# Next layer's modulation columns in the first feed-forward: another start, another order, one buffer

## The chip, the cores and the metric

The kernel runs on one core of a Trainium2 chip. The core has several engines with a queue of instructions each, worked off in order: TensorE (matrix products; PE in the profile, PEld for its weight loads), VectorE (DVE), ScalarE (ACT), GpSimd (POOL) and SyncE (SP, which here only issues transfers). Transfers between the large memory (HBM) and the on-chip memory run on 16 DMA engines, and are issued from the queues of SP and POOL. The metric is the time of one execution in microseconds (us), the median of several runs; smaller is better.

## The reference

Two layers of a diffusion backbone are computed for 512 latent tokens (x) and 256 context tokens (ctx), width 1024, in float32. Layer 0 mixes tokens by windowed attention, layer 1 by retention. Each layer ends with a gated feed-forward (SwiGLU, inner width 2816). Each layer is modulated: a condition vector is multiplied by a 1024 x 6144 matrix, and the six parts of the product shift, scale and gate the streams.

```python
for i in range(DEPTH):
    need_ctx_out = i < DEPTH - 1
    mx = jnp.split(c_act @ ada_w[i] + ada_b[i], 6, axis=-1)     # latent stream
    mc = jnp.split(cc_act @ ada_w[i] + ada_b[i], 6, axis=-1)    # context stream
    h_x = modulate(rms_norm(x, norm1_g[i]), mx[0], mx[1])
    h_c = modulate(rms_norm(y_ctx, norm1_g[i]), mc[0], mc[1])
    ...
    x = x + mx[2] * out_x
    x = x + mx[5] * swiglu(modulate(rms_norm(x, norm2_g[i]), mx[3], mx[4]), ffn_w_in[i], ffn_w_out[i])
```

In the last layer the context is not written any more. So layer 1 needs parts 0 and 1 (shift and scale ahead of the mixer) for both streams, and parts 2 to 5 for the latent stream alone. With 128 columns on the 128 partitions, a part is 8 columns of 128 values. That makes 16 columns for two streams and 32 for one.

## The kernel before

Activations lie with the width on the partitions. Each matrix product is done in three float32 products of split operands: a weight tile (128 x 1024 values, `wraw`) is rounded into a high part by a copy on ScalarE (`whi`, L165) and the rest is a subtraction on VectorE (`wlo`, L166, and L141 in `next_w`).

**The first feed-forward** (layer 0, L846 to L1085) works on both streams together, 768 tokens, as two halves of 384. Its inner width is cut into 22 tiles, f = 0 to 21, in groups of 2, 4, 4, 4, 4 and 4. The first two tiles are plain products. From f = 2 on `seven` computes a tile by seven products of half-size blocks instead of eight (L835, twelve matmuls of 384 columns each, into the banks X, Y and Z). Ahead of the products it prepares three pairs of split weights and one smaller pair (`bhi`, `blo`), with four additions on the raw weights (L960 to L966). Behind the products stand additions of the blocks (L977, L985, L987), the gate (L107, L908) and the split of the result (`act`, L165, L166).

After the first tile of a group, `output` multiplies the group before by the second weight matrix (L148 to L150): for each of the 8 blocks of 128 columns the latent stream into a bank `pj` and the context into a bank Z. VectorE adds the gated result to the stream (L253). The last group's `output` comes at the very end with `final` set, and also squares the streams for the next norm (L207 to L210).

**The modulation columns of layer 1** are computed on the side, by VectorE. `ada_tile` (L263) takes one column: POOL's queue issues the transfer of the column's weights (128 x 1024 values, 512 KB, L268). For each stream that needs it, one instruction on VectorE multiplies them by the activated condition row (`crow`: the first 1024 values for the latent stream, the second 1024 for the context) and sums along the row (L271, output `y`, a short readout of the sum behind it). A two-stream column has one transfer and two such reductions, a one-stream column one of each.

The columns wait in the list `ada_q`; `ada_next` (L946) takes one when called. It is called

- in `seven`, behind the split of its weights (from f = 3 on, when the condition rows are there),
- after `seven`, behind the split of its result, except in the first tile of a group,
- in an `output` that isn't final, after each second block of the latent stream, so four times.

That gives 4 calls in the output at f = 2, two each in f = 3, 4 and 5, and then in each group of four one in the first tile, four in its output and six in the three other tiles: 54 calls in all, for 48 columns.

**What sets the order.** The program is written for a framework that tracks which instruction needs which tile of memory, sets the waits, gives out buffers, and fixes the order of each engine's instructions when the program is built, by the order in which they are written and by a model of their times. `after` adds an edge that keeps an instruction behind another one on the same engine; each reduction has one, to the instruction named above. On the chip each engine then takes its instructions in that fixed order: if one waits, all behind it on that engine wait.

Memory is given out by name: `adaw` has one buffer in the pool of the feed-forward, so the next transfer into it can be issued only when the last reduction that reads the old weights is done. When fewer than 32 columns are left, and their number is odd, the weights go into the second half of `crow` instead, which is not read any more then. The same `adaw` buffer holds a weight part before (f = 1) and after (third weight tile of the final output, `spare_w`, L1001).

After the first feed-forward `fold_gain` (L114) joins parts of the modulation with the norms' gains for layer 1.

Of the kernel before, what the change touches and what calls it, by code (L numbers as in the profile page):

```python
# [16 lines left out]
KT = D // P  # L17
# [32 lines left out]
def dit_kernel(ctx, tc, xT, cT, crow, small, consts, masks, tabs0, tabs1, jtab, adaQ, adaN, adaT, wst, out):  # L50
# [11 lines left out]
    def T(pool, cols, tag, bufs, dt=F32):  # L62
        return pool.tile([P, cols], dt, tag=tag, bufs=bufs, name=tag)
# [27 lines left out]
    def after(ins, others):  # L91
        for o in others:
            tc.add_manual_dep(ins.ins, o.ins.name, order, reason="table set turn")
# [42 lines left out]
    def next_w(pool, own=2, raw=None):  # L136

        raw = raw or w_raw()
        hi, lo = w_parts(pool, own)
        nc.scalar.copy(hi, raw)  # L140
        nc.vector.tensor_tensor(lo, raw, hi, op=sub)  # L141
        return hi, lo
# [112 lines left out]
    def cond_rows(pool):  # L255

        cr = T(pool, 2048, "crow", 1)
        nc.sync.dma_start(cr, crow.broadcast_to([P, 2048]))
        for i in range(2):
            silu(cr[:, i * 1024:(i + 1) * 1024], cr[:, i * 1024:(i + 1) * 1024])  # L260
        return cr

    def ada_tile(l, part, d, streams, cr, behind, room, w=None):  # L263

        j = part * 8 + d
        if w is None:
            w = T(room, 1024, "adaw", 1 if l else 3)
        (nc.gpsimd if l else nc.sync).dma_start(w, adaT[l, j])  # L268
        for s in streams:
            junk = T(rp, 1024, "y0", 1, BF16) if l else T(room, 1024, "junk", 1, BF16)  # L270
            after(nc.vector.tensor_tensor_reduce(junk, w, cr[:, s * 1024:(s + 1) * 1024], 1.0,  # L271
                                                 sm_t[:, C_ADAB + l * 48 + j:C_ADAB + l * 48 + j + 1], mult, add,
                                                 mods[l, s][:, part, d:d + 1]), behind)
# [525 lines left out]
    cres = load_stream(1)  # L799
    At.close()  # L800
    AK.close()
    PLAIN = 2
    WIDE = SX + SC
    THIRDS = (slice(0, 384), slice(384, WIDE))
    E = ExitStack()
# [4 lines left out]
    for d4 in range(0, KT, 4):  # L810
        w = [next_w(wo_p) for _ in range(4)]
        if d4 == 0:
            cr = cond_rows(wo_p)
# [38 lines left out]
    fp = F.enter_context(tc.tile_pool(name="fp", bufs=1, reuse_waits="tile"))  # L852
# [42 lines left out]
    def last_sum():  # L895
        for k in range(4):
            S[4, k] = parts(quarter())
            split(park[:, k * 384:(k + 1) * 384], *S[4, k])
# [47 lines left out]

    def ada_next(behind):

        if ada_q:

            w = cr[:, 1024:2048] if len(ada_q) < 32 and len(ada_q) % 2 else None
            ada_tile(*ada_q.pop(0), cr, [behind], fp, w)

    def seven():
        g, u = raw_turn(), raw_turn()
# [13 lines left out]
        if cr:  # L969
            ada_next(half)  # L970
# [36 lines left out]
    def output(acts, final):  # L1007
        gsz = len(acts)
        nd = 1024 // (gsz * P)
        w = []  # L1010

        def one(s, res, c, d):
            while len(w) * nd <= d:
                w.append(spare_w() if final and len(w) == 2 else next_w(fp, 1, raw_turn()))
            wd = w[d // nd]
            o = bank("Z")[:, 0:SC] if s else pj()
            for k in range(gsz):
                c0 = k * nd * P + (d % nd) * P
                mm3(o, (wd[0][:, c0:c0 + P], wd[1][:, c0:c0 + P]),
                    (acts[k][:, c], acts[k][:, c.start + WIDE:c.stop + WIDE]), k == 0, k == gsz - 1)  # L1020
            ins = gated_add(s, 0, 5, d, o, res)
            if cr and not final and s == 0 and d % 2:
                ada_next(ins)
            if final:
                square_and_stats(s, d, res[d])

        if final:
            for st in streams:
                for d in range(KT):
                    one(*st, d)  # L1030
        else:
            for d in range(KT):
                for st in streams:
                    one(*st, d)
# [7 lines left out]
            nc.sync.dma_start(w[k], adaN[u, k // 2][:, k % 2 * 512:k % 2 * 512 + 512])  # L1042
        return ada_unit(u, w, pj, columns)

    ada_q = [(1, part, d, (0, 1)) for part in (0, 1) for d in range(KT)]
    ada_q += [(1, part, d, (0,)) for part in (2, 3, 4, 5) for d in range(KT)]
    wsel[0] = 0
    raws = [0]
    cr = None
# [5 lines left out]
    f, prev = 0, None  # L1055
    for gsz in FFN_GROUPS:
        acts = []
        for i in range(gsz):
            if f < PLAIN:
                acts.append(first[f])  # L1060
                if f == 1:
                    ends.pop(0)()
            else:
                if f == PLAIN:
                    last_sum()
                a, end = seven()
                acts.append(a)
                if f == PLAIN:
                    ends.pop(0)()
                    cr = cond_rows(fp)  # L1070
                if i or f == PLAIN + 2:
                    ada_next(end)
            if i == 0 and prev is not None:
                output(prev, False)
            f += 1
        prev = acts
# [181 lines left out]
    for hd in range(RH):  # L1258
# [211 lines left out]
        w = []  # L1470
# [70 lines left out]
    fp = F.enter_context(tc.tile_pool(name="fp", bufs=1, reuse_waits="tile"))  # L1541
# [88 lines left out]
    f, prev = 0, None  # L1630
    for gsz in FFN_GROUPS:
        acts = []
        for i in range(gsz):
            if f < 2:
                acts.append(first[f])
            elif f == 2:
                w = [next_w(fp), next_w(fp)]
# [153 lines left out]
```

## Time and profile before

| What | us |
|---|---|
| Time, median of 3 runs | 1789.98 |
| lowest and highest run | 1786.59 and 1791.28 |
| Span of the profiled execution | 1794.1 |
| busy in it: PE, VectorE, ScalarE, POOL | 1728.8, 1357.8, 841.7, 134.9 |
| one reduction of a modulation column, mean | 1.279 |

The page gives no time of the profiled execution beside its span; the span lies 4.1 us above the median of the three runs. The profile has several views. The page names the busy time of each engine. The windows view gives busy time by stretch of the span, with the granted clock of TensorE (PEclk, 1.00 is full). The groups of instructions give the line, the engine, what is written from what, how many; busy time and mean; and then the engine's idle time just before them with the instruction that ended it (`<-`). The timeline has single instructions: start, duration, engine, line, and in brackets the idle time before and what ended it. The chain of waits follows the work that ended last back from step to step, with the start and length of each. Times are us from the start of the span unless marked as ns.

### The profile page before, as it was taken

What the parts mean: (1) busy time and instruction counts of PE and PEld (TensorE: products, weight loads), DVE (VectorE), ACT (ScalarE), POOL (GpSimd) and SP (SyncE); (2) the same over time, 40 slices, a digit from 0 to 9 for tenths busy, and PEclk for the clock granted to TensorE, in tenths of its full rate; (3) what the DMA queues carried; (4) which work ended last, traced back from release to release, by engine and by line L of the source; (5) the groups of instructions that cost most, each with busy time, mean ns of one, the idle gap of its engine ahead of it and who ended that gap; (6) DMA issues with size and microseconds to landing.
All of it is one profiled execution on the core that took longest, in us unless ns stands there. A gap on an engine that the chain in (4) does not pass through costs nothing.

```text
span 1794.1 us, 27599 instructions
## 1 busy us (share of the span) xinstructions
PE 1728.8 (96%) x10852; PEld 1535.8 (86%) x10852; DVE 1357.8 (76%) x2365; ACT 841.7 (47%) x1477; POOL 134.9 (8%) x275
## 2 busy tenths in 40 slices
PE   6899999999989999999999999999999999999999
PEld 4777776789889999999988788888897899999998
DVE  6697777688878868686689867758758798777774
ACT  5476666456232425252455534534524465445432
POOL 0035334000000000000010000000000000000000
PEclk9999999999999999999999999999999999999999
DMA  9510002434444534342233533434433323333322
GB/s 339 228 36 25 24 1 83 150 108 154 124 125 130 162 107 153 118 153 83 83 107 106 166 105 110 162 95 134 152 115 117 96 71 106 95 112 112 89 89 83
DMA packets 59890, 206.68 MB, mean 115 GB/s; under 512 B 6640, under 2 KB 7024, under 8 KB 59504
## 3 DMA queue, kind: packets, MB, share of 16 engines
q1 hardware_dynamic: 52848, 179.75, 31.3%
q0 software_dynamic: 6912, 25.17, 4.6%
q8 instruction: 85, 1.39, 0.3%
q14 instruction: 45, 0.37, 0.1%
HBM read 202.80 MB, written 2.10 MB: 114 GB/s over the span
## 4 chain that ended last, share of the span: by engine, by line
PE 73%; DVE 12%; DMA 6%; ACT 4%; issue 2%; POOL 2%; SPq 0%; ACTq 0%; DVEq 0%; POOLq 0%
PE Y L835 13%; PE Z L835 6%; PE pj L148 6%; PE pj L150 6%; PE pj L149 6%; PE Y L1180 4%; PE Z L1193 4%; PE X L835 3%; DMA wraw<-in_wst_dram 2%; DVE wlo L166 2%; PE pj L1193 2%; PE pT L707 2%; DMA adaw<-in_adaT_dram 2%; PE pO L719 2%; PE S L684 2%
## 5 line engine op out<-in xcount | busy, mean ns | idle before, releaser
L165 ACT CAST whi<-wraw 128x1024 fp32r<-128x1024 f32 x177 | 185.1, 1050 | 286.0 <-PE Z L150 70.3
L166 DVE TENSOR_TENSOR wlo<-wraw,whi 128x1024 fp32r<-128x1024 f32 x177 | 215.9, 1222 | 43.4 <-ACT whi L165 43.4
L835 PE MATMUL Y<-aq,whi 128*128 128x384 f32 x640 | 175.6, 338 | 6.1 <-ACT whi L165 4.1
L253 DVE SCALAR_TENSOR_TENSOR res<-pj,mod,res 128x512 f32<-128x512 f32 (+1 forms) x112 | 81.5, 729 | 69.5 <-PE pj L150 68.6
L141 DVE TENSOR_TENSOR wlo<-wraw,whi 128x1024 fp32r<-128x1024 f32 x80 | 98.1, 1227 | 38.0 <-ACT whi L140 37.3
L835 PEld LDWEIGHTS Y<-aq,whi 128*128 128x128 f32 x640 | 117.6, 189 | 8.2 <-ACT whi L165 5.1
L140 ACT CAST whi<-wraw 128x1024 fp32r<-128x1024 f32 x80 | 84.0, 1050 | 81.6 <-DMA wraw<-in_wst_dram 26.8
L835 PE MATMUL Y<-aq,wlo 128*128 128x384 f32 x320 | 108.0, 338 | 1.1 <-DVE wlo L166 1.1
L101 ACT ACTIVATE pr<-pr,stat,qs 128x513 f32<-128x513 f32 (+2 forms) x96 | 74.2, 775 | 31.7 <-DVE stat L691 30.9
L1193 PE MATMUL Z<-whi,sA 128*128 128x512 f32 x256 | 81.0, 392 | 0.6 <-ACT whi L165 0.6
L698 POOL TENSOR_SCALAR pr<-pr,stat 128x512 f32<-128x512 f32 (+2 forms) x96 | 67.2, 714 | 88.8 <-DVE stat L695 66.5
L271 DVE CUSTOM_DVE_ANT_0 y<-adaw,crow,small_sb 128x1024 bf16<-128x1024 f32 x48 | 61.4, 1279 | 12.0 <-DMA adaw<-in_adaT_dram 12.0
L148 PE MATMUL pj<-ax,whi 128*128 128x512 f32 x176 | 68.7, 390 | 0.2 <-DVE res L253 0.2
L150 PE MATMUL pj<-ax,whi 128*128 128x512 f32 x176 | 68.7, 390 | 0.0
L149 PE MATMUL pj<-ax,wlo 128*128 128x512 f32 x176 | 68.5, 389 | 0.0
L707 PE MATMUL pT<-const_sb,pr 128*128 128x128 f32 x352 | 58.8, 287 | 9.9 <-POOL pr L698 7.6
L148 PE MATMUL pj<-act,whi 128*128 128x512 f32 x168 | 66.5, 396 | 0.5 <-DVE res L253 0.5
L149 PE MATMUL pj<-act,wlo 128*128 128x512 f32 x168 | 65.9, 392 | 0.0
L150 PE MATMUL pj<-act,whi 128*128 128x512 f32 x168 | 65.5, 390 | 0.0
L707 PEld LDWEIGHTS pT<-const_sb,pr 128*128 128x128 f32 x352 | 39.6, 142 | 30.2 <-POOL pr L698 18.5
L685 DVE CUSTOM_DVE_ANT_0 pr<-S,mask,qs 128x256 f32<-128x256 f32 (+1 forms) x96 | 53.1, 567 | 15.3 <-PE S L684 8.9
L835 PEld LDWEIGHTS Y<-aq,wlo 128*128 128x128 f32 x320 | 60.6, 189 | 1.8 <-DVE wlo L166 1.8
(520 smaller groups left out, 5277.3 us busy)
## 6 DMA issues: line engine op xcount, KB each, us to landing
wraw<-in_wst_dram SPq DMA_DIRECT2D x238, 512.0 KB, 3.6
adaw<-in_adaT_dram POOLq DMA_DIRECT2D x32, 512.0 KB, 4.3
wx<-in_wst_dram SPq DMA_DIRECT2D x24, 512.0 KB, 4.6
adan<-in_adaQ_dram SPq DMA_DIRECT2D x16, 512.0 KB, 7.5
adan<-in_adaN_dram SPq DMA_DIRECT2D x16, 512.0 KB, 8.8
crow<-in_adaT_dram POOLq DMA_DIRECT2D x16, 512.0 KB, 4.4
res<-in_xT_dram SPq DMA_DIRECT2D x16, 256.0 KB, 5.6
adaw<-in_adaT_dram SPq DMA_DIRECT2D x8, 512.0 KB, 4.1
```

The costliest lines, as they stand in the source:

```text
L101: ins = nc.scalar.activation(*args, **kw)
L140: nc.scalar.copy(hi, raw)
L141: nc.vector.tensor_tensor(lo, raw, hi, op=sub)
L148: nc.tensor.matmul(o, whi, xhi, start=first, stop=False)
L149: nc.tensor.matmul(o, wlo, xhi, start=False, stop=False)
L150: return nc.tensor.matmul(o, whi, xlo, start=False, stop=last)
L165: nc.scalar.copy(hi, t)
L166: return nc.vector.tensor_tensor(lo, t, hi, op=sub)
L253: return nc.vector.scalar_tensor_tensor(res[d], o, mods[l, s][:, part, d:d + 1], res[d], mult, add)
L707: nc.tensor.transpose(tp[:, a * P:(a + 1) * P], self.pr[(0, 2, 1, 3)[a]][:, ki * P:(ki + 1) * P], ident)
L835: nc.tensor.matmul(o, p, r, start=first and k + i == 0, stop=k == 3 and i == 2, skip_group_check=not first)
L1193: ins = nc.tensor.matmul(o, p, r, start=first and k + i == 0, stop=k == 3 and i == 2, skip_group_check=not first)
```

## The change

Three things change in the first feed-forward; the columns computed stay the same 48.

1. `ada_next` does nothing while f < 4. Of the 54 calls, the four in the output at f = 2 and the two in f = 3 fall away; 48 are left, and the last column is taken behind f = 21, just ahead of the final output.
2. The list is filled in another order: not 16 two-stream columns and then 32 one-stream ones, but sixteen times two one-stream columns (parts 2 to 5) and one two-stream column (parts 0 and 1). The last column of the list is a two-stream one.
3. All columns use the buffer `adaw`; none goes to the second half of `crow`, which the context reductions now read until the end.

```diff
-    PLAIN = 2
+    PLAIN, ADA_FROM = 2, 4
...
     def ada_next(behind):
 
-        if ada_q:
-
-            w = cr[:, 1024:2048] if len(ada_q) < 32 and len(ada_q) % 2 else None
-            ada_tile(*ada_q.pop(0), cr, [behind], fp, w)
+        if ada_q and f >= ADA_FROM:
+            ada_tile(*ada_q.pop(0), cr, [behind], fp)
...
-    ada_q = [(1, part, d, (0, 1)) for part in (0, 1) for d in range(KT)]
-    ada_q += [(1, part, d, (0,)) for part in (2, 3, 4, 5) for d in range(KT)]
+    ada_q = []
+    for i in range(2 * KT):
+        ada_q += [(1, 2 + (2 * i + e) // KT, (2 * i + e) % KT, (0,)) for e in range(2)]
+        ada_q.append((1, i // KT, i % KT, (0, 1)))
```

## The prediction

> **What bounds the kernel now.** I read the page first: its busy shares name TensorE, so the question is where TensorE is not busy.
>
> ```profile
> span 1794.1 us, 27599 instructions
> PE 1728.8 (96%) x10852; PEld 1535.8 (86%) x10852; DVE 1357.8 (76%) x2365; ACT 841.7 (47%) x1477; POOL 134.9 (8%) x275
> ```
>
> A share over the whole span hides stages, so next I cut the first feed-forward into stretches: 440 to 531 us holds the first output and the tiles f = 3 to 6, 531 to 841 the rest of the modulation work, 841 to 889 the last tiles, in which no modulation column is left.
>
> ```profile
> core 0: us, PE busy (x) PEld busy (x) DVE busy (x) ACT busy (x) POOL busy (x), PEclk, DMA share, GB/s
> 440.00:531.00 91.00, 81.98 (x440) 75.76 (x439) 75.43 (x120) 32.78 (x53) 5.29 (x10) 0.96 0.37 114
> 531.00:577.00 46.00, 46.00 (x266) 42.13 (x265) 39.55 (x62) 11.73 (x16) 3.17 (x6) 1.00 0.37 120
> 577.00:841.00 264.00, 264.00 (x1520) 252.17 (x1520) 200.07 (x300) 96.44 (x149) 16.41 (x31) 1.00 0.44 134
> 841.00:889.00 48.00, 48.00 (x274) 47.09 (x273) 31.39 (x45) 24.18 (x38) 0.00 (x0) 1.00 0.27 77
> ```
>
> From 531 us on PE is busy in every microsecond: nothing can be gained there, only lost. In the first stretch it is idle for 91.00 - 81.98 = 9.0 us, and there the clock is below 1. Who ends those gaps, by groups of PE instructions in that stretch:
>
> ```profile
> L835 PE MATMUL Y<-aq,whi 128*128 128x384 f32 x128 | 37.0, 350 | 6.1 <-ACT whi L165 4.1 <-ACT hn L975 1.5 <-ACT sq L984 0.4
> L835 PE MATMUL Y<-aq,wlo 128*128 128x384 f32 x64 | 22.5, 351 | 1.1 <-DVE wlo L166 1.1
> L835 PE MATMUL Z<-aq,whi 128*128 128x384 f32 x35 | 10.0, 344 | 1.3 <-ACT sq L982 1.3
> L148 PE MATMUL pj<-act,whi 128*128 128x512 f32 x18 | 7.7, 426 | 0.5 <-DVE res L253 0.5
> L271 DVE CUSTOM_DVE_ANT_0 y<-adaw,crow,small_sb 128x1024 bf16<-128x1024 f32 x20 | 25.6, 1280 | 7.0 <-DMA adaw<-in_adaT_dram 7.0
> ```
>
> 6.1 + 1.1 + 1.3 + 0.5 is all of the 9.0. The names are ScalarE and VectorE, but ScalarE is 36% busy in the stretch (32.78 of 91.00), so it is late because its own inputs are. The last row is VectorE's: 20 modulation reductions, 25.6 us of work, and 7.0 us in which VectorE stood still for the modulation weights. The chain of waits, in order of time, shows one link of it:
>
> ```profile
> 504.81 1.20 DVE y L271
> 506.31 6.68 DMA adaw<-in_adaT_dram
> 513.01 1.28 DVE y L271
> 514.30 0.47 DVE sq L985
> 514.77 1.20 DVE y L271
> 516.27 3.94 DMA adaw<-in_adaT_dram
> 520.23 1.28 DVE y L271
> 521.53 1.15 DVE wlo L166
> 522.72 0.69 PE Y L835
> ```
>
> Two reductions end, only then is the one buffer refilled, VectorE runs into the next reduction and waits in order, and the weight split (wlo) that TensorE needs stands behind it. What the wait costs on PE:
>
> ```profile
> 519.85 0.44 PE L835 MATMUL Y<-aq,whi 128*128 128x384 f32 x1 [2.65 <-ACT whi L165]
> 521.58 0.69 PE L835 MATMUL Z<-aq,whi 128*128 128x384 f32 x1 [1.30 <-ACT sq L982]
> 520.50:527.20 6.70, 5.17 (x15) 4.67 (x16) 5.64 (x7) 2.46 (x5) 0.53 (x1) 0.51 0.40 111
> ```
>
> After gaps of 2.65 and 1.30 us the granted clock is 0.51 for 6.7 us. PE was busy for 5.17 us of that; at full clock the same work takes 5.17 x 0.51 = 2.6, so 2.5 us more are lost.
>
> **The change part by part.** *The late start.* No column is taken before f = 4. That removes from the first output (f = 2) four columns and from f = 3 two, all for two streams: 12 reductions at 1280 ns, 15.4 us of VectorE, and six transfers on POOL's queue, which all come later instead. The other four columns of the stretch (f = 4 and f = 5, eight reductions) become one-stream columns in three cases. Without any reduction VectorE's work in the stretch is 75.43 - 25.6 = 49.8 us; f = 4 and f = 5 put back 1 + 1 + 2 + 1 = 5 reductions, 6.4 us (f = 6 one more). That is 56 us of work beside 80 us of TensorE work, so the cover is there. Of the 9.0 idle us I count 8.6 as going: the 0.4 behind sq L984 stays, since it comes from the activation of the condition rows, ahead of it on ScalarE and waiting for its own transfer. With the gaps the drop of the clock goes, 2.5. Gain 11.1.
>
> ```profile
> 439.69 2.01 ACT L107 ACTIVATE crow<-crow 128x1024 f32<-128x1024 f32 x2 [2.33 <-DMA crow<-in_crow_dram]
> ```
>
> What is late next there? The weight transfers: in the same stretch VectorE also waited once for a raw weight.
>
> ```profile
> DVE wraw L960 <- DMA wraw<-in_wst_dram: 1.8, 1, 1.8
> ```
>
> It may show again; between nothing and half of the 9.0 (4.5) of the idle may stay, and I take 1.0, nearer the lower end, since a single 1.8 us wait on VectorE is all that the rows show beside the modulation.
>
> *The mixed order, and 48 calls up to the end.* Total reductions stay 64, transfers 48. They now go at 4/3 reductions a call instead of one (before: two, then one), and six columns fall on f = 19 to 21, where none was (eight reductions, 10.2 us). In a tile of two calls (f = 4, 5, and the three after each output) there are two or three reductions. Before, with two:
>
> ```profile
> 581.15:595.71 14.56, 14.56 (x86) 14.56 (x85) 12.90 (x20) 7.33 (x12) 1.06 (x2) 1.00 0.51 147
> 581.15:595.71 14.56, 2.58 (x4) 1.00 0.51 147
> 624.87:658.29 33.42, 33.42 (x193) 29.49 (x192) 22.93 (x35) 5.62 (x7) 1.59 (x3) 1.00 0.37 110
> ```
>
> The first row is one seven-product tile, 14.56 us of unbroken PE with VectorE at 12.90; the second is the reductions alone, 2.58 for two. A third brings VectorE to 14.2, still under 14.56. Three such tiles after an output hold eight reductions at most: 3 x 12.90 + 2 x 1.29 = 41.3 of 43.7. The third row is an output: four calls and 22.93 of 33.42, where 1.3 reductions more do nothing. How far may VectorE be late inside a tile? The tight place is the weight split after the last product:
>
> ```profile
> 593.63 4.16 PE Y L835 x24
> 599.87 2.08 PE Y L835 x12
> 597.27 1.23 DVE L166 TENSOR_TENSOR wlo<-wraw,whi 128x1024 fp32r<-128x1024 f32 x1 [0.34 <-ACT whi L165]
> 598.88 1.28 DVE L271 CUSTOM_DVE_ANT_0 y<-adaw,crow,small_sb 128x1024 bf16<-128x1024 f32 x1
> ```
>
> That split ends at 598.5 and PE uses it at 599.87: 1.4 us to spare, with the reduction behind it. So I take the arithmetic of the mixing as hidden: 0, bounds 0 and 3 us (0.25 for each of the twelve tight tiles).
>
> *One buffer.* The second place (the unused half of the condition rows) goes. POOL's queue then waits at every column for the reduction before it, and the only other work of that queue comes in the final output. VectorE waits only if it comes to a reduction before its transfer has landed.
>
> ```profile
> adaw<-in_adaT_dram POOLq DMA_DIRECT2D x16, 512.0 KB, 3.9
> DMA to landing us min/median/max: 3.7/4.4/7.4
> ```
>
> The first row is for 445 to 577 us, the second for 577 to 832. From the end of a reduction to the issue it takes 0.3 us (506.00 to 506.31 above), so a turn is 4.7 us at the median. Two calls in a tile: 2 x 4.7 + 2.67 x 1.29 + 0.2 for the instruction within a pair = 13.0 us of 14.56. With two-stream columns alone, as before: 2 x 4.2 + 4 x 1.28 + 2 x 0.47 = 14.5, even with the shorter landing: that is why the early stretch was bound by this chain, and the mixed order isn't. Cost 0 at the median; it is the first rival's price above it.
>
> *The end.* A pair of reductions now lies between the last tile and the final output.
>
> ```profile
> 888.07 0.55 DVE L166 TENSOR_TENSOR act<-sq,act 128x384 fp32r<-128x384 f32 x1
> 889.28 0.75 DVE L253 SCALAR_TENSOR_TENSOR res<-pj,mod,res 128x512 f32<-128x512 f32 x1 [0.66 <-PE pj L150]
> 889.95 1.22 DVE L166 TENSOR_TENSOR adaw<-wraw 128x1024 fp32r<-128x1024 f32 x1
> 891.12 0.75 DVE L253 SCALAR_TENSOR_TENSOR res<-pj,mod,res 128x512 f32<-128x512 f32 x1
> 578.96 0.24 DVE L114 SCALAR_TENSOR_TENSOR acol<-mod,gm 128x8 f32<-128x8 f32 x2
> ```
>
> The pair (2.6 us) can begin when the split at 888.07 is through, and end at 891.2. If it goes ahead of the gated add at 889.28, that is late by 1.9 us, and its bank was wanted for the third column block about 891: up to 1.5 us of PE. If it goes behind, nothing. I take 0.8, the middle. The last row is the next layer's folded gains, done at 579 us before; they now wait for this last pair: two instructions, 0.24 us, during the final output, after which they are first used.
>
> **Sum.** 8.6 + 2.5 - 1.0 - 0 - 0 - 0.8 = 9.3 us less: 1794.1 becomes 1784.8 in the profiled execution. That execution lies 4.1 us above the median of the runs shown (1789.98), so I carry the difference: 1780.7.
>
> On the clock, the Trainium skill ("TensorE: Matmul & The Clock Gate", Part 1) says that TensorE falls to half clock after about one idle window of 3.4 us and needs a busy one to come back. The trace agrees in kind: 3.95 us of gaps with one matmul between, then 0.51. By the page one window at half clock costs an estimated 1.7 us instead of 2.5, and the sum would be 8.5.
>
> **The rivals.** *The single buffer becomes the bound (slower).* Place: the 14 tiles with two calls. For it: the 6.68 us transfer above, a turn of 7.0 with its issue, and the 7.0 us of waits with this same buffer. Against it: both medians, and that the two-stream columns from 531 to 577 us, on one buffer, cost PE nothing (46.00 of 46.00). With a turn x the cycle is 2x + 3.6; it passes 14.56 at x = 5.5. My gain is used up near 5.8, slower by over 0.3% needs 6.0. At 6.3 it is 16.2, so 1.64 x 14 = 23 us: 1804.
>
> The Trainium skill ("Trainium Kernel Development and Optimization", Best Practices) advises double-buffering to overlap transfers with computing. It speaks against this part; the trace bears it out for two-stream columns in tiles of seven products (7.0 us), not between outputs.
>
> *The gap moves instead of closing.* f = 4 to 6 still use the single buffer, with three reductions in f = 5, and weights for f = 4 come no sooner. If half the idle stays (4.5), no matmul gap reaches the length that dropped the clock, sevens lose 1.5 and the end 1.0: 11.1 - 7.0 = 4.1 less, 1785.9, within what can be told from no change. For it: DMA already served f = 4 late once (1.8 us). Against it: VectorE has 24 us of room.
>
> *The early gap isn't due to the modulation at all,* only labelled so because those reductions happen to stand in order there: then nothing is gained, and the end and the sevens cost 0.8 to 3: 1791 to 1793. Against it stands the chain, in which a landing releases every second link.
>
> **How the numbers follow.** 0.3%, some 5.4 us, is about what a measurement of this kernel can tell from no change. Likeliest case 0.71 (1777 to 1784.5 by its own bounds: 11.1 gained and a run spread of 2, against 4.5 - 1.0 more left over); gap moved 0.12; not due 0.04; single buffer 0.13, mostly over 1795. So faster 0.71, same 0.16, slower 0.13. The range reaches from 1776 to 1789: it takes in the moved gap and leaves out the slow rival and the third.
>
> **What would show it.** Right: PE without gaps over 0.5 us from 443 us to the end of the first feed-forward, clock 1.00 there, VectorE 55 to 60 us busy in the 80 us after 440, the final output beginning about 10 us earlier. The first part is wrong if PE gaps between the first output and tile 7 still sum to over 4 us; the mixing and the one buffer are wrong if VectorE's idle time before the reductions exceeds some 10 us in total and PE has gaps after 531 us; the end, if PE has a gap over 1.5 us in the final output.

## The result and the profile after

| | before | changed |
|---|---|---|
| median of 4 runs each | 1790.63 us | 1778.32 us |
| lowest and highest | 1786.59 and 1793.67 | 1777.24 and 1782.69 |
| ratio, with its 95% interval | | 0.9935 (0.9915 to 0.9956) |
| profiled execution: time, span | span 1794.1 | 1777.24, 1775.5 |

The change makes the kernel 12.3 us faster by the medians; 9.3 were forecast. The page of the changed kernel begins:

```profile
span 1775.5 us, 27602 instructions
PE 1717.1 (97%) x10852; PEld 1527.1 (86%) x10852; DVE 1356.0 (76%) x2365; ACT 841.2 (47%) x1477; POOL 134.4 (8%) x275
```

VectorE does the same work (1356.0 against 1357.8), PE has the same 10852 matmuls. By stretches, the same three as before and the 80 us for which the prediction named a load:

```profile
core 0: us, PE busy (x) PEld busy (x) DVE busy (x) ACT busy (x) POOL busy (x), PEclk, DMA share, GB/s
440.00:531.00 91.00, 90.99 (x522) 87.08 (x522) 70.80 (x107) 34.61 (x56) 3.17 (x6) 1.00 0.35 109
531.00:577.00 46.00, 46.00 (x270) 44.00 (x269) 37.27 (x56) 15.51 (x24) 3.17 (x6) 1.00 0.34 106
577.00:841.00 264.00, 263.15 (x1514) 250.65 (x1513) 207.53 (x314) 94.33 (x147) 16.36 (x31) 1.00 0.43 132
440.00:520.00 80.00, 79.99 (x462) 77.51 (x462) 64.09 (x97) 33.56 (x55) 2.65 (x5) 1.00 0.34 104
```

In the first row the 9.0 us of idle PE and the low clock are gone, and the number in brackets says more than the busy time: 522 matmuls start in these 91 us, where 440 did before. In the third row PE now has 0.85 us of gaps, where it had none. The groups of VectorE's instructions from 430 to 880 us show what the single buffer does:

```profile
L271 DVE CUSTOM_DVE_ANT_0 y<-adaw,crow,small_sb 128x1024 bf16<-128x1024 f32 x64 | 81.9, 1279 | 33.7 <-DMA adaw<-in_adaT_dram 33.5
```

VectorE stands still for modulation weights for 33.5 us, against 12.0 on the page before. The waits are up to 5.6 us long; here are two, one early and one late, from the timeline (start, duration, and in brackets the idle time):

```profile
513.33 1.28 DVE L271 CUSTOM_DVE_ANT_0 y<-adaw,crow,small_sb 128x1024 bf16<-128x1024 f32 x1 [4.55 <-DMA adaw<-in_adaT_dram]
790.94 1.28 DVE L271 CUSTOM_DVE_ANT_0 y<-adaw,crow,small_sb 128x1024 bf16<-128x1024 f32 x1 [5.58 <-DMA adaw<-in_adaT_dram]
```

PE has no gap behind either of them. So the waits grew almost threefold, and the kernel is faster; the experiments below test whether what counts is how far VectorE is ahead when it waits.

**One clock for all kernels.** Each trace here holds the same 10852 matmuls, and the same ones lie between the numbers used here, so they can be numbered by their start, and the time between two numbers compared. From number 3001 to 3601 runs the early stretch (the end of f = 2 to about the output behind f = 6), from 3601 to 5501 the rest of the tiles, from 5501 to 5701 the end of the last tile and the final output up to the next layer's first norm. Lost is what is over the shortest time in any kernel (104.77, 329.75 and 37.01 us).

| kernel | early, us | lost | later, us | lost | end, us |
|---|---|---|---|---|---|
| before | 119.49 | 14.72 | 329.75 | 0.00 | 37.03 |
| changed | 104.94 | 0.17 | 331.47 | 1.72 | 37.16 |
| changed, again | 105.11 | 0.34 | 330.18 | 0.43 | 37.02 |
| late start only | 104.97 | 0.20 | 331.89 | 2.14 | 37.03 |
| late start only, again | 106.31 | 1.54 | 330.46 | 0.71 | 37.03 |
| mixed order only | 108.44 | 3.67 | 330.99 | 1.24 | 37.03 |
| start at f = 3, old order | 106.87 | 2.10 | 331.15 | 1.40 | 37.02 |
| before, no transfers | 109.66 | 4.89 | 329.75 | 0.00 | 37.02 |
| before, short reductions | 105.11 | 0.34 | 329.75 | 0.00 | 37.01 |
| changed, no transfers | 104.78 | 0.01 | 329.75 | 0.00 | 37.03 |
| changed, start at f = 3 | 104.85 | 0.08 | 330.46 | 0.71 | 37.01 |
| two streams in outputs | 104.78 | 0.01 | 329.75 | 0.00 | 37.03 |
| two streams in outputs, again | 104.77 | 0.00 | 329.75 | 0.00 | 37.03 |

By this count the change gains 14.55 us early and gives back 1.72 later and 0.13 at the end: 12.7, near the 12.3 of the medians. The two spans differ by more, 18.6. 2.5 of the rest lie ahead of number 3001 and 3.4 behind 5701, where the work is the same but for the transfer of the first column. Such shifts come and go between executions: the kernel with two streams in outputs reached number 3001 at 432.7 us in one profile and at 426.1 in the other.

One thing more differs between the kernels: the order of TensorE's matmuls, fixed when the program is built. Of the 2700 positions from 3001 to 5700, 246 hold a matmul of another product in the kernel before than in the changed one, all of them in the early stretch, where single matmuls of later products are drawn forward. The kernel with short reductions has the changed kernel's order, the one without transfers an order of its own. The mixed order alone loses 3.67 us early though it differs from the changed kernel in only 36 positions. No run changes TensorE's order alone, so what it costs by itself stays open.

### The profile page after: what moved, and what is told of

Same layout as the page of the kernel before. It is cut to its first block, busy times and chain, and to the rows that moved or that the text cites. A ratio compares the mean times of both kernels' runs of the same rounds, so it can differ in the third digit from the quotient of the medians.

```text
span 1775.5 us, 27602 instructions
## 1 busy us (share of the span) xinstructions
PE 1717.1 (97%) x10852; PEld 1527.1 (86%) x10852; DVE 1356.0 (76%) x2365; ACT 841.2 (47%) x1477; POOL 134.4 (8%) x275
## 4 chain that ended last, share of the span: by engine, by line
PE 74%; DVE 13%; ACT 4%; DMA 4%; issue 2%; POOL 2%; SPq 0%; ACTq 0%; DVEq 0%; POOLq 0%
PE Y L835 13%; PE Z L835 6%; PE pj L148 6%; PE pj L150 6%; PE pj L149 6%; PE Y L1180 4%; PE Z L1193 3%; PE X L835 3%; DVE wlo L166 3%; DMA wraw<-in_wst_dram 2%; PE pT L707 2%; PE S L684 2%; PE pO L719 2%; PE pj L1193 2%; PE X L1180 1%
## 5 line engine op out<-in xcount | busy, mean ns | idle before, releaser
L271 DVE CUSTOM_DVE_ANT_0 y<-adaw,crow,small_sb 128x1024 bf16<-128x1024 f32 x64 | 81.9, 1279 | 33.7 <-DMA adaw<-in_adaT_dram 33.5
L268 POOL DMA_DIRECT2D adaw<-in_adaT_dram x48 | 25.6, 533 | 520.6 <-DVE mod L271 420.8
```

## The experiments

Times are compared as ratios to the kernel before on the same chip; its median was 1791.86 us beside the first four kernels, 1788.24 beside the next four, 1787.53 beside the last three.

### The late start alone

```diff
-        if ada_q:
+        if ada_q and f >= 4:
```

> Only the late start: no column before f = 4, with the old list (16 two-stream columns first) and the old second place. Theory (start and mixed order both count): the gaps of the first output and f = 3 close, but two-stream columns now stand in f = 4, 5, 7, 8 and 9, with four reductions in a tile, 15.5 us of VectorE in 14.56 of TensorE, and a turn of the single buffer of 4.2 to 4.7 us twice; 1 to 2 us lost in each of the five. Expected 3 to 9 us faster than before, TensorE gaps of 5 to 10 us in those tiles. Rival (only the first output and f = 3 matter, the order is worth nothing): 11 to 13 us faster, no gaps after 531 us.

Measured: 1777.66 us, ratio 0.9919 (0.9907 to 0.9931). By stretches, and PE's waits from 430 to 900 us:

```profile
440.00:531.00 91.00, 91.00 (x526) 86.98 (x524) 74.78 (x116) 34.73 (x55) 3.19 (x6) 1.00 0.36 110
531.00:577.00 46.00, 46.00 (x267) 44.16 (x266) 41.17 (x66) 16.02 (x25) 3.18 (x6) 1.00 0.34 105
577.00:841.00 264.00, 262.74 (x1510) 249.93 (x1509) 201.81 (x303) 95.56 (x148) 16.96 (x32) 1.00 0.43 134
PE Y L835 <- DVE wlo L166: 1.1, 1, 1.1
PE Y L835 <- ACT hn L975: 0.2, 1, 0.2
```

The expectation was wrong in its main point: two-stream columns in f = 4 and f = 5 cost nothing measurable in this profile. One gap of 1.1 us and some tenths came at 597 us, early in f = 10, right behind three tiles with four reductions each. So four reductions in a tile do not cost 1 to 2 us each; that they use up a lead first is tested below. The rival (the order is worth nothing) comes nearer: the medians differ by 14.2 us, above its 11 to 13, but a gap after 531 us, which it excluded, is there.

### The mixed order alone, on one buffer

```diff
-            w = cr[:, 1024:2048] if len(ada_q) < 32 and len(ada_q) % 2 else None
-            ada_tile(*ada_q.pop(0), cr, [behind], fp, w)
+            ada_tile(*ada_q.pop(0), cr, [behind], fp)
...
-    ada_q = [(1, part, d, (0, 1)) for part in (0, 1) for d in range(KT)]
...
+    for i in range(2 * KT):
+        ada_q += [(1, 2 + (2 * i + e) // KT, (2 * i + e) % KT, (0,)) for e in range(2)]
+        ada_q.append((1, i // KT, i % KT, (0, 1)))
```

> Only the mixed order on the one buffer, with columns from the first output (f = 2) on as before. Theory: in the first output five reductions instead of eight, about 17 us of VectorE beside 16.8 of TensorE, in f = 3 two or three; 2 to 4 us of TensorE are still lost there. Expected 8 to 11 us faster than before. Rival (the start alone counts): 0 to 3 us faster, with gaps of 8 us or more before 531 us.

Measured: 1780.38 us, ratio 0.9945 (0.993 to 0.996). The early stretch, and the only waits of PE from 430 to 905 us:

```profile
440.00:531.00 91.00, 88.67 (x506) 83.83 (x505) 77.45 (x121) 33.33 (x54) 6.37 (x12) 1.00 0.43 136
PE Y L835 <- ACT hn L974: 2.9, 4, 1.0
```

3.67 us are lost early, as expected, 2.33 of them shown as idle in three gaps of 0.6 to 1.0 us; the fourth wait in the row comes later, at 782 us. The clock stays at 1.00. The mixing alone, with the columns in the first output, brings four fifths of what the late start brings.

### Transfers or work: the kernel before without one, and without the other

```diff
-        (nc.gpsimd if l else nc.sync).dma_start(w, adaT[l, j])
+        if not (l and kept):
+            (nc.gpsimd if l else nc.sync).dma_start(w, adaT[l, j])
+        if l and not kept:
+            kept.append(w)
```

with `w = kept[0]` for the columns behind the first.

> The kernel before, with the transfer of the first column alone: all 64 reductions stay at their places and read that one column's weights, so the columns 2 to 48 of layer 1's modulation are not computed from their own weights. This takes away each wait for the buffer and leaves VectorE's work. Theory A (the turn of the buffer is what delays the splits): the early gaps close but for 1 to 3 us, 10 to 13 us faster than before. Rival B (VectorE's work itself, 25.6 us of reductions in 91 us, is too much there): more than half of the early loss stays, 0 to 6 us faster.

The second keeps the transfers and cuts each reduction of layer 1 to 32 values:

```diff
-            after(nc.vector.tensor_tensor_reduce(junk, w, cr[:, s * 1024:(s + 1) * 1024], 1.0,
+            n = 32 if l else 1024
+            after(nc.vector.tensor_tensor_reduce(junk[:, :n], w[:, :n], cr[:, s * 1024:s * 1024 + n], 1.0,
```

> The kernel before, with all transfers, but each reduction of layer 1 over 32 of the 1024 values (the columns are then not the whole sums). This takes away VectorE's work of the columns and leaves every transfer, the single buffer and its order. Theory A (the turn of the buffer): VectorE still stands for landings of 4 us, a turn of 4.7 twice in 14.56 us fits, so half of the gain, 5 to 9 us. Rival B (VectorE's work): all of the early loss goes, 11 to 15 us faster.

Measured: 1781.86 us without transfers, ratio 0.9938 (0.9926 to 0.9951); 1779.08 us with short reductions, 0.9925 (0.9913 to 0.9937). The stretch from 440 to 531 us and the reductions in it, first without transfers:

```profile
440.00:531.00 91.00, 88.59 (x498) 82.48 (x497) 85.35 (x135) 33.66 (x54) 0.00 (x0) 1.00 0.24 71
L276 DVE CUSTOM_DVE_ANT_0 y<-adaw,crow,small_sb 128x1024 bf16<-128x1024 f32 x24 | 30.7, 1278 | 0.1
```

and then with short reductions:

```profile
440.00:531.00 91.00, 90.76 (x521) 86.81 (x520) 66.53 (x141) 35.30 (x57) 6.37 (x12) 1.00 0.47 145
L272 DVE CUSTOM_DVE_ANT_0 y<-adaw,crow,small_sb 128x32 bf16<-128x32 f32 x24 | 6.0, 249 | 9.7 <-DMA adaw<-in_adaT_dram 9.4
```

Without a single wait for the columns' weights VectorE is 94% busy (85.35 of 91.00) and 4.89 us are lost: the work alone is too much in this place. With 9.4 us of waits, but little work, 0.34 is lost: waits for the buffer alone cost next to nothing (the short reductions shorten its turn as well). So theory A, as I put it, falls: the buffer does not delay the splits by itself. Its time for the missing transfers did come (10.0 us by the medians), but 4.89 us lost are more than its 1 to 3. Rival B is right for the short reductions (12.8 us) and wrong for the missing transfers, which brought 9.8 us of the 14.7. The full loss needs both the reductions and the transfers; whether the transfers count by the waits or also by the load on the DMA engines (share 0.24 without them, 0.37 before) is not separated. 4.9 for the work, 7.0 of waits (the row in the prediction) and 2.5 for the low clock would be 14.4 of 14.7; that this is how they add up is arithmetic, not shown.

### Without the first output's columns

```diff
-        if ada_q:
+        if ada_q and f >= 3:
```

> The kernel before, but no column in the first output (f = 2): the list starts at f = 3, in the old order with the old second place. Theory (a debt: VectorE falls behind over several tiles in a row, 4 us in the first output and about 1 us of work and 1 us of waits in each of f = 3, 4, 5): without the first output's eight reductions VectorE goes into f = 3 with a lead of about 6 us, so TensorE loses 4 us at most before the output at f = 6; 9 to 13 us faster than before. Rival (each tile with two two-stream columns on the one buffer loses 2 to 3 us by itself): 6 to 9 us are still lost there, 4 to 8 us faster.

Measured: 1782.05 us, ratio 0.9957 (0.9943 to 0.9972), so some 8 us; by the count of matmuls 2.10 us are lost early and 1.40 later, 11.2 less than before. The early stretch and PE's largest waits from 430 to 905 us:

```profile
440.00:531.00 91.00, 89.33 (x513) 85.26 (x512) 80.00 (x126) 35.82 (x57) 4.24 (x8) 1.00 0.37 110
PE Y L835 <- ACT hn L975: 1.5, 1, 1.5
PE Y L835 <- DVE wlo L166: 0.9, 1, 0.9
```

f = 3, 4 and 5 carry the same two two-stream columns each, on the same buffer, as in the kernel before; only the four columns of the first output are gone ahead of them, and 12.6 of the 14.7 us early loss with them. The one early gap over 0.5 us comes at 506 us, early in f = 6. That is the debt: a tile with four reductions loses nothing while VectorE has a lead, and here, as in the first profile of the late start alone, the lead out of an output lasts for three such tiles. The lead can be read from the trace, as the time from the end of the middle one of a tile's three weight splits to the first matmul that reads it; here for f = 5 and f = 6:

```profile
490.10 1.23 DVE L166 TENSOR_TENSOR wlo<-wraw,whi 128x1024 fp32r<-128x1024 f32 x1 [0.30 <-ACT whi L165]
492.21 0.33 PE L835 MATMUL Y<-aq,wlo 128*128 128x384 f32 x1
506.51 1.23 DVE L166 TENSOR_TENSOR wlo<-wraw,whi 128x1024 fp32r<-128x1024 f32 x1 [0.18 <-ACT whi L165]
508.55 0.34 PE L835 MATMUL Y<-aq,wlo 128*128 128x384 f32 x1
```

It shrinks from 6.6 us in f = 3 and 3.9 in f = 4 to 0.9 and 0.8 here. In the kernel before it is 0.1 to 0.3 in all of f = 3 to 6: there each of these splits ends just as TensorE wants it. In the changed kernel it is 6.6, 3.9, 3.9 and 2.2. The rival (2 to 3 us in each tile) falls by the matmul count; the medians (6 us by their difference, 8 by the ratio) are under the expected 9 and inside the rival's 4 to 8, and would not decide it.

### The changed kernel without transfers

The edit is the one above, in the changed kernel.

> The changed kernel with the transfer of the first column alone; the reductions stay and read that one column's weights, so the later columns are not computed from their own. VectorE's 33.5 us of waits for the one buffer go. Theory (they lie beside TensorE's work, which lost 1.3 us in the tiles and some tenths at the end): 1 to 2 us faster than the changed kernel, TensorE without gaps over 0.3 us between 437 and 870 us. Rival (the single buffer costs several us that the lead only hides in part): 4 us or more faster than the changed kernel.

Measured: 1776.59 us, ratio 0.9931 (0.9918 to 0.9943), against 0.9935 (0.9915 to 0.9956) and, again, 0.9934 (0.9921 to 0.9946) for the changed kernel.

```profile
577.00:841.00 264.00, 264.00 (x1522) 252.17 (x1521) 208.24 (x314) 96.23 (x148) 0.00 (x0) 1.00 0.23 70
```

All gaps are gone: by the count of matmuls the transfers cost the changed kernel 1.9 us in one profile and 0.8 in the other. The medians cannot tell that. Whether it is the wait for the buffer or the load that these transfers put on the DMA engines stays open, since both are gone here; the gap at 597 us, one of the two over 0.3 us, follows a late weight transfer, as five links (others lie between them) from the chain of waits of the changed kernel show:

```profile
582.55 5.82 DMA wraw<-in_wst_dram
588.47 0.70 DVE wraw L958
589.81 1.28 DVE y L271
597.21 0.48 ACT hn L973
597.73 2.39 PE Y L835 x12
```

### Start at f = 3, mixed order

```diff
-    PLAIN, ADA_FROM = 2, 4
+    PLAIN, ADA_FROM = 2, 3
```

> The changed kernel with the start at f = 3 instead of 4: two calls more, so the last column falls two calls earlier and none stands between the last tile and the final output. Theory (debt): f = 3 is carried by the lead out of the first output, no gap there; the 0.3 us at the final output's start go: within 1 us of the changed kernel, or up to 1 us faster. Rival (f = 3 is what must be kept free): a gap of 1 us or more between 455 and 510 us, 1 to 4 us slower than the changed kernel.

Measured: 1778.79 us, ratio 0.9945 (0.9933 to 0.9958). Early 0.08 us lost, later 0.71, the end 37.01 us. The lead carries f = 3, as the theory has it; against the changed kernel no difference can be told.

### Two-stream columns in the outputs

```diff
-            ada_tile(*ada_q.pop(0), cr, [behind], fp)
+            ada_tile(*q.pop(0), cr, [behind], fp)
...
-                ada_next(ins)
+                ada_next(ins, both)
```

`both` is the list of the 16 two-stream columns, taken by the 16 calls of the outputs; `ada_q` holds the 32 others for the calls in the tiles.

> Start at f = 4, but each two-stream column is taken by a call of an output (16 of them) and each one-stream column by a call in a tile (32): never more than two reductions in a tile of 14.56 us, eight in an output of 33.4 us. Theory: VectorE is nowhere over TensorE, so no gaps over 0.3 us in the tiles: 0.5 to 2 us faster than the changed kernel, 13 to 15 us faster than before. Rival (the turn of the single buffer decides, not the number of reductions): gaps as in the changed kernel, no difference from it.

Measured: 1777.74 us, ratio 0.9934 (0.9921 to 0.9948).

```profile
440.00:531.00 91.00, 91.00 (x523) 87.46 (x522) 68.06 (x105) 38.34 (x60) 2.65 (x5) 1.00 0.36 109
577.00:841.00 264.00, 264.00 (x1522) 252.17 (x1521) 210.79 (x320) 95.05 (x147) 16.89 (x32) 1.00 0.42 132
DVE y L271 <- DMA adaw<-in_adaT_dram: 25.0, 14, 3.7
```

No gap is left from the first output to the last tile, with 25.0 us of waits for the one buffer still there. So the turn of the buffer alone makes no gap. The number of reductions in a tile alone does not either: without transfers the gaps vanished at the changed kernel's own number. The time can't be told from the changed kernel's, and the expected 13 to 15 us are not met: 10.5 by the medians, 11.8 by the ratio.

### Three of them again, on one chip

> The changed kernel again, on one chip with the next two. 0.6 to 0.75% faster than before; TensorE gaps of 1 to 2.5 us in the tiles after 531 us, as in its first profile.

> Two-stream columns in the outputs, one-stream ones in the tiles, again. Theory: no gap over 0.3 us in the tiles again, so 1 to 3 us faster than the changed kernel on the same chip. Rival (the gaps are worth nothing at the end, or vary from run to run): within 0.5 us of it.

> The late start alone, again. Theory: one or two gaps of 1 to 2 us in f = 8 or 9, four reductions a tile; within 1 us of the changed kernel. Rival (the old second place is worth something): 1.5 us or more faster than the changed kernel.

Measured: 1774.78 us for the changed kernel, ratio 0.9934 (0.9921 to 0.9946); 1775.56 with two streams in outputs, 0.9931 (0.9918 to 0.9943); 1775.24 with the late start alone, 0.9934 (0.992 to 0.9947). The gaps came out smaller than expected in the changed kernel (0.77 us early and later together) and differ from run to run: the late start alone lost 1.54 us early this time, in a gap at 503 us, early in f = 6 and so behind only two tiles with four reductions, and 0.20 the first time, though the middle split of f = 6 was 0.8 us ahead of its use in both; its second gap was again in f = 10. The kernel with two streams in outputs was without a gap both times, but a microsecond or two is not to be told from these medians, and the expectation of 1 to 3 us is not met. None of the kernels tried is measurably faster than the changed one.

## Why the prediction was right, and where it was off

The time was 1778.3 for a forecast of 1780.7, the gain 12.3 for 9.3.

*The early gap: right in place and cause, undersized.* The prediction counted 8.6 us of idle time and 2.5 of low clock as going. 14.55 went. The step that failed is the reading of a gap as its idle time: a matmul that stands alone is shown busy for 0.34 to 0.69 us in the rows below (the profile models these ends), though in a stream the next one starts 0.17 us after it. The two rows quoted there lie between these two of the kernel before:

```profile
516.86 0.34 PE L835 MATMUL Z<-aq,bhi 128*128 128x384 f32 x1
522.72 0.69 PE L835 MATMUL Y<-aq,wlo 128*128 128x384 f32 x1 [0.45 <-DVE wlo L166]
```

From 516.86 to 522.72 us three matmuls started, which at the pace of 2.08 us for twelve take 0.52; so 5.34 us were lost, and the idle times noted are 2.65 + 1.30 + 0.45, that is 4.40 (part of the rest is the low clock, which the 2.5 count too). Over the early stretch the nine gaps take 11.0 us more from start to start than the pace, where 9.0 are shown as idle; 2.3 more lie in the matmuls from 522.72 to 527.45 us, at the low clock, and about 1.4 in later starts of under 0.2 us each, shown as busy. The 82 matmuls that the stretch gained, at about 0.17 us each, are 14 us, the right size. That one row of the windows (440 against 522) would have needed the changed trace; but the work of the stretch, counted in matmuls times pace, could have been set against its 91 us from the trace of before.

*What may stay there, 1.0:* 0.17 stayed, 0.34 in the second profile. The 0.4 that the prediction left standing behind the condition rows is gone as well: PE is busy for 14.99 of the 15.00 us from 430 to 445. The raw weight that was late once, ahead of f = 6 and not of f = 4 as the prediction has it, did not show again early.

*VectorE's cover:* forecast were 55 to 60 us of VectorE in 80 after 440; it was 64.09. The reductions there are six, about as counted; more of the other work fell there, with 462 matmuls in these 80 us against 440 in the 91 of before, and PE was still whole: 79.99 of 80. The final output began 15.4 us earlier (869.86 for 885.21), for about 10.

*The mixed order and one buffer, 0 with bounds 0 and 3:* 1.72 and 0.43 us were lost in the later tiles. The size is inside the bounds. But the sign by which the prediction would call this part wrong, more than 10 us of VectorE's waits together with PE gaps after 531 us, did come: the waits are 33.5 us, and PE has gaps of 0.37 and 0.47 us. As a sign of harm it was set too low, since they cost under 2 us. The turn was sized well (3.9 us to landing at the median, 6.8 at most); what was missed is that VectorE comes early to many reductions, and waits there with time in hand.

*The mixing as the reason that the chain lets go:* wrong. The prediction held that two-stream columns alone bind the chain (14.5 us of 14.56) and the mixed order frees it. The late start alone, with the old order, gains as much, and its four reductions and two transfers in each of f = 4 and f = 5 fit their tiles. What differs is the lead: in the kernel before VectorE comes into these tiles with none (0.1 to 0.3 us).

*The end, 0.8 with bounds 0 and 1.5:* 0.13 us, and nothing in the second profile. The pair of reductions went between the gated adds, as the timeline of the changed kernel shows:

```profile
873.19 1.28 DVE L271 CUSTOM_DVE_ANT_0 y<-adaw,crow,small_sb 128x1024 bf16<-128x1024 f32 x1
874.40 0.74 DVE L253 SCALAR_TENSOR_TENSOR res<-pj,mod,res 128x512 f32<-128x512 f32 x1
875.06 1.27 DVE L271 CUSTOM_DVE_ANT_0 y<-adaw,crow,small_sb 128x1024 bf16<-128x1024 f32 x1
876.26 0.74 DVE L253 SCALAR_TENSOR_TENSOR res<-pj,mod,res 128x512 f32<-128x512 f32 x1
876.93 1.22 DVE L166 TENSOR_TENSOR adaw<-wraw 128x1024 fp32r<-128x1024 f32 x1
```

*The rivals.* The single buffer as the bound did not come, though its sign, long waits on VectorE, did. The gap did not move. That it had another cause than the modulation is excluded by the short reductions, with which 0.34 us of the loss is left. The rule of the Trainium skill ("Trainium Kernel Development and Optimization", Best Practices) to double-buffer would have spoken against the change; here the second place shows no worth that can be measured: the changed kernel and the late start alone, which keeps it, are at 1774.78 and 1775.24 us on one chip, though these two differ in the order as well, and no run takes away the second place alone. The estimate from the Trainium skill's page "TensorE: Matmul & The Clock Gate" (1.7 us, for one window at half clock) is too low for the kernel before: the row shows 0.51 for 6.7 us, about two such windows, and the matmuls behind the last gap alone took the 2.3 us named above. The low clock did not return when the gaps went.

## What to carry to other kernels

Side work on an engine that is nearly full does harm by the sum over several tiles in a row: look for the stretch where its load is over the bound engine's, and move the work out of that stretch, rather than trim each wait. A wait on a side engine costs only what its lead doesn't cover; 33.5 us of waits cost under 2 here, while in the early stretch of the kernel before, where the lead was gone, 7.0 us of them stood beside a loss of 14.7, of which 9.8 went with the transfers. And count the bound engine's instructions in a stretch beside its idle time, since a busy share overstates an engine that works in single steps.

## What was not expected

That 0.94 us of a 5.86 us stretch without a stream was shown as busy PE, as worked out above, and that the early loss (14.7 us) was 3.2 us over the sum of the idle time and the low clock in the profile. And that the kernel with two streams in outputs ran 434.5 us of tiles to within 0.01 us of the same time in two profiles, 104.77 and 329.75, though VectorE waited for 25.0 us in the one and 19.7 in the other: the matmul stream hides all of it.
